# Start addresses of the matmuls' moving operands in a three-stage decoder layer: two groups of tiles are placed elsewhere

## The chip, the core and the metric

The kernel runs on one core of one Trainium2 chip, as one launch. The metric is the device time of a launch in microseconds; less is better. Engines are named as in the profile: PE is the matrix engine (PEld its weight loads), DVE the vector engine, ACT the scalar engine, POOL the general one, SP the queue that issues the loads.

## What is computed

One layer on 16 learned tokens and 256 tokens of x, width 2048, all in float32:

```
hs = concat(meta_tokens, x)                                   # 272 x 2048
f  = (silu(rms(hs) @ w_gate) * (rms(hs) @ w_up)) @ w_down      # first block, inner width 5632
hs = hs + 0.5 * rms(f)
m  = concat(sparse_attention(rms(hs) @ w_in), gated_linear_attention(rms(hs) @ w_in)) @ w_out
hs = hs + rms(m)
f  = (silu(rms(hs) @ w_gate2) * (rms(hs) @ w_up2)) @ w_down2   # second block
hs = hs + 0.5 * rms(f);  output hs[16:]                        # 256 x 2048
```

(Each rms has its own gain.) The weights are read once, some 356 MB.

## The kernel before

**Precision.** Each float32 operand is split into a rounded upper part and a lower rest (`hi`, `lo`), both float32r. A product takes three matmuls: upper weights with upper x, lower weights with upper x, upper weights with lower x (`mm3`, L137 to L141, for most of the first block and the mixer). ACT writes the upper part, DVE the lower one (`split`).

**Weights.** `load` fetches a 512 x 512 piece (1 MB) into one of three `raw` tiles over SP's queue and splits it into two `whi` and two `wlo` tiles of 4096 bytes in each partition, five buffers each. In the gate, up, input and output projections and in the first block's down projection, the weights are the stationary operand: 128 columns of 512 bytes, taken at `f * 512` bytes and `(k % 2) * 2048` bytes of such a tile. All `whi`, `wlo` and `raw` tiles begin at 96 modulo 256 bytes in their partition.

**x.** The normed activations, transposed, lie in one tile `xg` of 34816 bytes in each partition, at address 36704. For the first block and the input projections it holds 16 chunks of 272 tokens, each as 272 upper and 272 lower values, so one row of moving values is 1088 bytes and rows start 1088 bytes apart (`xs`). From the output projection on, only the 256 real tokens are needed, and `xn2` lays 16 chunks of 256 upper and 256 lower values over the same tile, `XOFF` elements from its start: rows of 1024 bytes, 1024 bytes apart (`xs2`).

**First block.** For each of 11 slices of 512 inner columns, `gate_up` (L531) streams w_gate and w_up against `xg` (272 columns a matmul), multiplies silu(gate) and up, and leaves four pairs `hhi`, `hlo` of 128 x 272; eight buffers each, so that two slices are alive. `down1` then runs w_down against them: for 16 output chunks, 4 x 3 matmuls with 272 columns, `hhi`, `hhi`, `hlo` for k = 0 to 3 (L139, L140, L141).

**Mixer.** `stream_pair` (L216) runs two index projections at once, chunk by chunk, 256 columns a matmul (L255, L256, L258, and one more of 272 columns for small weights at the end of each row of them); `stream_block` runs the others. Where 256 tokens are enough (`n == NX`, L188), upper weights meet upper and lower x in one matmul of 512 columns (L197, four in a row for k = 0 to 3), and lower weights meet upper x in one of 256 columns (L199, four in a row). With `xs`, the two halves of such a 512 are 1088 bytes apart; with `xs2` they lie end to end.

**Output projection and second block.** Both read x through `xs2`: the output projection and ten slices of gate and all but the first of up by L197 and L199, the first slice of gate and up by `stream_pair`, the last 128 output columns of the output projection by `mm3` with 256 columns. `down2` has the weights as moving operand: 512 columns of `whi`, `whi`, `wlo` against `hhi`, `hlo` (L1066 to L1068).

**Order.** The PE's order is the order of the code, written out by hand; small matmuls of the mixer are put between the large ones by a `Background` of tasks with costs. ACT and DVE are ordered by the framework.

Of the kernel before, what the change touches and what calls it, by code (L numbers as in the profile page):

```python
# [8 lines left out]
F32 = mybir.dt.float32  # L9
F32R = mybir.dt.float32r  # L10
# [5 lines left out]
P = 128  # L16
D = 2048
KC = D // P

XOFF = 64  # L20
FF = 5632
NM = 16
NX = 256
# [55 lines left out]
def layer_kernel(ctx: ExitStack, tc: tile.TileContext, a: dict, out: bass.AP):  # L79
# [130 lines left out]
    def joined(dst, bank):  # L210

        h = st.tile([P, T], F32, name="sqt", bufs=3)
        act.activation(h[:, :NX], bank[:, NX:], AF.Copy)
        return dve.tensor_tensor(dst, bank[:, :NX], h[:, :NX], op=ALU.add)
# [68 lines left out]

    xn2 = xg.rearrange("p c s t -> p (c s t)")[:, XOFF:XOFF + KC * 2 * NX]
    xn2 = xn2.rearrange("p (c s t) -> p c s t", c=KC, s=2)
# [64 lines left out]
    def sqrt_table(after):  # L350

        j = st.tile([P, 1], F32, name="junk1", bufs=1)
        act.activation(j, after, AF.Sqrt, bias=eps, scale=0.0)
# [178 lines left out]
    def gate_up(pool_, wg, wu, b, xs, sl, r, first, how=None):  # L532

        n = sl.stop - sl.start
        pair = first is not None and n == NX
        banks = first or stream_block(wg, b * BW, xs, sl, how=how)
        sg = []
        for f in range(4):
            t1 = pool_.tile([P, n], F32, name="gr", bufs=2)
            if n == NX and not first:  # L540
                joined(t1, banks[f])
                dve.tensor_tensor(t1, t1, r[:, :n], op=ALU.mult)
            else:
                dve.tensor_tensor(t1, banks[f][:, :n], r[:, :n], op=ALU.mult)
            s = pool_.tile([P, n], F32, name="sg", bufs=4)
            act.activation(s, t1, AF.Silu)
            sg.append(s)
        if b == NB - 1:
            sqrt_table(sg[3][:, 0:1])
        banks = [x[:, NX:] for x in first] if pair else stream_block(wu, b * BW, xs, sl)  # L550
        hid = []
        for f in range(4):
            if n == NX and not pair:
                t1 = pool_.tile([P, n], F32, name="gr", bufs=2)
                joined(t1, banks[f])
                dve.tensor_tensor(sg[f], t1, sg[f], op=ALU.mult)
            else:
                dve.tensor_tensor(sg[f], banks[f][:, :n], sg[f], op=ALU.mult)
            hi = pool_.tile([P, n], F32R, name="hhi", bufs=8)
            lo = pool_.tile([P, n], F32R, name="hlo", bufs=8)  # L560
            act.activation(hi, sg[f], AF.Copy)
            dve.tensor_tensor(lo, sg[f], hi.bitcast(F32), op=ALU.subtract)
            hid.append((hi, lo))
        return hid
# [44 lines left out]
    for b in range(NB):  # L609
        if b == NB - 1:  # L610

            w_in = a["w_in"]
            small_w = mixp.tile([P, 2, KC, P], F32R, name="mix")
            raw = wp.tile([P, KC, P], F32, name="raw", bufs=3)
            pool.memset(raw[:, :, 64:128], 0.0)
            for c0, n, o in ((C_IK, 80, 0), (C_GL, 16, 96)):
                nc.sync.dma_start(out=raw[:, :, o:o + n],
                                  in_=w_in[:, c0:c0 + n].rearrange("(k p) c -> p k c", p=P))
            for j in range(2):
                js = slice(8 * j, 8 * j + 8)  # L620
                split(raw[:, js], small_w[:, 0, js], small_w[:, 1, js])
        hid = gate_up(fp, a["ffn1_w_gate"], a["ffn1_w_up"], b, xs, full, begin.r, first if b == 0 else None)
        if prev is not None:
            down1(b - 1, prev)
        prev = hid
# [422 lines left out]
    with tc.tile_pool(name="ffn2", bufs=1) as fp:  # L1048
# [69 lines left out]
        for b in range(NB):  # L1118
            if b == 1:
                natural = bg.add(natural_task())  # L1120
                sums = ssf[:, 0], fp.tile([P, 8], F32, name="sse")
            hid = gate_up(fp, a["ffn2_w_gate"], a["ffn2_w_up"], b, xs2, alone, bound.r, first if b == 0 else None,
                          bound.how_next if b == 1 else None)
            if prev is not None:
                down2(b - 1, prev)
            prev = hid
# [28 lines left out]
```

## Time and profile before

| what | us |
|---|---|
| median of 3 runs (2078.28 to 2079.88) | 2079.64 |
| the profiled execution | 2079.47 |
| its span, first to last instruction | 2077.5 |
| PE busy (99% of the span) | 2060.6 |
| PEld busy | 1920.6 |
| DVE busy | 1269.1 |
| ACT busy | 942.4 |

How to read it: 2 us of the profiled execution lie outside its span. Busy time of PE counts a matmul from its start to a modelled end, and matmuls overlap: one of 272 columns is shown with 0.29 us, while the next starts some 0.125 us after it. What one costs the core is therefore the distance from its start to the next one's start. The views print starts to 0.01 us; the trace holds them to 1 ns. Means given with a count are means of those distances over all matmuls of the line with the named start address.

### The profile page before, as it was taken

To read this page: it belongs to the slowest core of one execution; us is meant where nothing else is said; L and a number is where in the kernel's file an instruction comes from. 1 tells how busy PE (TensorE), PEld (TensorE's weight loads), DVE (VectorE), ACT (ScalarE), POOL (GpSimd) and SP (SyncE) were. 2 spreads that over 40 slices of the span, in tenths; PEclk is the share of its full clock that TensorE was granted. 3 is DMA by queue.
4 is the path that set the end of the run, shared out by engine and by line. 5 is a ranking of instruction groups with operands and counts; after the bars stand their busy time and mean duration, and the time that the engine had idled before them with its cause. 6 is when DMAs were issued, how large, how long until landed. Compare 5 with 4: busy or idle time off the path is not lost.

```text
span 2077.5 us, 33335 instructions
## 1 busy us (share of the span) xinstructions
PE 2060.6 (99%) x13988; PEld 1920.6 (92%) x13988; DVE 1269.1 (61%) x1900; ACT 942.4 (45%) x1347; POOL 20.6 (1%) x36
## 2 busy tenths in 40 slices
PE   9999999999999999999999999999999999999998
PEld 9999999999999999989989998998888888888886
DVE  6455555545555657878764455776656566566657
ACT  6333433433333344664544455564444444444443
POOL 3000000000000000000000000000000000000000
PEclk9999999999999999999999999999999999999999
DMA  7555555555555654444444445465655655555653
GB/s 247 167 178 176 170 182 168 178 178 168 182 169 176 195 166 142 159 147 142 156 133 139 143 161 163 162 203 184 196 188 183 194 190 185 192 191 185 200 183 122
DMA packets 184648, 360.71 MB, mean 174 GB/s; under 512 B 9919, under 2 KB 10513, under 8 KB 184354
## 3 DMA queue, kind: packets, MB, share of 16 engines
q1 hardware_dynamic: 183552, 356.41, 52.5%
q8 instruction: 110, 1.80, 0.4%
q10 hardware_dynamic: 786, 2.14, 0.3%
q14 instruction: 40, 0.33, 0.0%
q0 software_dynamic: 160, 0.03, 0.0%
HBM read 356.46 MB, written 2.10 MB: 173 GB/s over the span
## 4 chain that ended last, share of the span: by engine, by line
PE 95%; issue 2%; DVE 1%; ACT 1%; DMA 0%; POOLq 0%; DVEq 0%; POOL 0%; ACTq 0%
PE mmb L197 20%; PE mmb L141 15%; PE mmb L139 15%; PE mmb L140 15%; PE mmb L199 10%; PE mmb L1067 4%; PE mmb L1066 4%; PE mmb L1068 4%; PE mmb L255 2%; PE mmb L256 2%; PE mmb L258 2%; PE axb L877 0%; DVE wlo L107 0%; PE axb L812 0%; PE mmb L183 0%
## 5 line engine op out<-in xcount | busy, mean ns | idle before, releaser
L107 DVE TENSOR_TENSOR wlo<-raw,whi 128x1024 fp32r<-128x1024 f32 (+1 forms) x674 | 805.2, 1218 | 582.1 <-ACT whi L106 581.0
L106 ACT ACTIVATE whi<-raw 128x1024 fp32r<-128x1024 f32 (+1 forms) x674 | 684.5, 1050 | 793.9 <-PE mmb L141 416.3
L139 PE MATMUL mmb<-xg,whi 128*128 128x272 f32 (+1 forms) x1808 | 525.0, 290 | 0.2 <-DVE qk L653 0.2
L141 PE MATMUL mmb<-xg,whi 128*128 128x272 f32 (+1 forms) x1808 | 522.0, 289 | 0.0
L140 PE MATMUL mmb<-xg,wlo 128*128 128x272 f32 (+1 forms) x1808 | 519.3, 287 | 0.0
L197 PE MATMUL mmb<-xg,whi 128*128 128x512 f32 x1840 | 506.2, 396 | 0.0
L197 PEld LDWEIGHTS mmb<-xg,whi 128*128 128x128 f32 x1840 | 314.9, 189 | 46.5 <-issue 4.0
L139 PEld LDWEIGHTS mmb<-xg,whi 128*128 128x128 f32 x1808 | 339.6, 188 | 4.8 <-issue 3.6
L141 PEld LDWEIGHTS mmb<-xg,whi 128*128 128x128 f32 x1808 | 340.5, 188 | 0.0
L140 PEld LDWEIGHTS mmb<-xg,wlo 128*128 128x128 f32 x1808 | 339.8, 188 | 0.2
L199 PEld LDWEIGHTS mmb<-xg,wlo 128*128 128x128 f32 x1840 | 281.8, 188 | 39.3
L199 PE MATMUL mmb<-xg,wlo 128*128 128x256 f32 x1840 | 292.1, 280 | 0.0
L141 PE MATMUL mmb<-hlo,whi 128*128 128x272 f32 x704 | 204.1, 290 | 0.0
L139 PE MATMUL mmb<-hhi,whi 128*128 128x272 f32 x704 | 203.8, 289 | 0.0
L140 PE MATMUL mmb<-hhi,wlo 128*128 128x272 f32 x704 | 202.0, 287 | 0.0
L1068 PE MATMUL mmb<-wlo,hhi 128*128 128x512 f32 (+1 forms) x356 | 137.8, 387 | 0.0
L1067 PE MATMUL mmb<-whi,hlo 128*128 128x512 f32 (+1 forms) x356 | 137.8, 387 | 0.0
L1066 PE MATMUL mmb<-whi,hhi 128*128 128x512 f32 (+1 forms) x356 | 137.7, 387 | 0.0
L139 PEld LDWEIGHTS mmb<-hhi,whi 128*128 128x128 f32 x704 | 133.1, 189 | 0.0
L141 PEld LDWEIGHTS mmb<-hlo,whi 128*128 128x128 f32 x704 | 132.7, 188 | 0.0
L140 PEld LDWEIGHTS mmb<-hhi,wlo 128*128 128x128 f32 x704 | 132.5, 188 | 0.0
L603 DVE TENSOR_TENSOR acc<-mmb,acc 128x272 f32<-128x272 f32 x160 | 70.2, 439 | 72.2 <-PE mmb L141 71.5
(265 smaller groups left out, 1611.2 us busy)
## 6 DMA issues: line engine op xcount, KB each, us to landing
raw<-in_ffn_w_up_dram SPq DMA_DIRECT2D x88, 1024.0 KB, 5.1
raw<-in_ffn_w_down_dram SPq DMA_DIRECT2D x88, 1024.0 KB, 5.1
raw<-in_ffn_w_gate_dram SPq DMA_DIRECT2D x87, 1024.0 KB, 5.1
raw<-in_w_in_dram SPq DMA_DIRECT2D x56, 1024.0 KB, 5.0
raw<-in_w_out_dram SPq DMA_DIRECT2D x16, 1024.0 KB, 5.0
xn<-in_x_dram SPq DMA_DIRECT2D x3, 512.0 KB, 8.3
raw<-in_ffn_w_gate_dram SPq DMA_DIRECT2D x4, 256.0 KB, 4.9
grep<-in_ffn_post_g_dram ACTq DMA_DIRECT2D x1, 1024.0 KB, 4.8
```

The source lines that it names most:

```text
L106: for ins, prior in zip((act.activation(hi, raw, AF.Copy), eng.tensor_tensor(lo, raw, hi.bitcast(F32), op=ALU.subtract)), after):
L107: eng.tensor_tensor(lo, raw, hi.bitcast(F32), op=ALU.subtract)), after):
L139: pe.matmul(ps, whi, xhi, start=start, stop=False)
L140: pe.matmul(ps, wlo, xhi, start=False, stop=False)
L141: pe.matmul(ps, whi, xlo, start=False, stop=stop)
L197: pe.matmul(wide, hi, x[k], start=ui == 0 and k == 0, stop=False)
L199: pe.matmul(wide[:, 0], wof(k, f)[1], x[k][:, 0], start=False, stop=ui == 3 and k == 3)
L255: pe.matmul(ps, hi, xh, start=c == 0 and own, stop=False, skip_group_check=True)
L603: dve.tensor_tensor(acc[:, c], ps[:, :T], acc[:, c], op=ALU.add)
L1066: pe.matmul(ps, hh[:, tk], whi, start=k == 0, stop=False)
L1067: pe.matmul(ps, hl[:, tk], whi, start=False, stop=False)
L1068: pe.matmul(ps, hh[:, tk], wlo, start=False, stop=k == 3)
```

## The change

Three places are edited. `XOFF` goes from 64 to 48 elements, so all of `xn2` lies 64 bytes lower within `xg`. In the first block (and there alone, `n != NX`) the `hhi` and `hlo` tiles are allocated with 320 elements of which 272 are used, and the two `gr` tiles with 280.

```
-XOFF = 64
+
+XOFF = 48
...
-            t1 = pool_.tile([P, n], F32, name="gr", bufs=2)
+            t1 = pool_.tile([P, n if n == NX else n + 8], F32, name="gr", bufs=2)[:, :n]
...
-            hi = pool_.tile([P, n], F32R, name="hhi", bufs=8)
-            lo = pool_.tile([P, n], F32R, name="hlo", bufs=8)
+            hi, lo = (pool_.tile([P, n if n == NX else 320], F32R, name=x, bufs=8)[:, :n] for x in ("hhi", "hlo"))
```

Start addresses in a partition, modulo 256 bytes, in the two built programs:

| operand | before | after |
|---|---|---|
| moving `hhi` and `hlo` of the first block, k = 0, 1, 2, 3 | 224, 160, 96, 32 (both alike) | 32, 32, 32, 32 |
| moving rows of `xn2` (upper and lower) | 96 | 32 |
| moving rows of `xg` through `xs`, 272 columns: upper of even, odd chunks | 96, 224 | same |
| the same, lower of even, odd chunks | 160, 32 | same |
| moving 256 tokens of `xg` through `xs`: upper of even, odd chunks | 160, 32 | same |
| the same, lower of even, odd chunks | 224, 96 | same |
| stationary `whi`, `wlo` | 96 | same |
| moving `whi`, `wlo`, stationary `hhi`, `hlo` in `down2` | 96 | same |
| the four `sg` tiles of the first block | 224, 32, 96, 160 | 32, 96, 160, 224 |
| the two `gr` tiles of the first block | 96, 160 | 96, 192 |

No instruction is added, removed or moved on any engine, and the number and sizes of the loads are the same. One wait goes: DVE writes the lower part of `xn2` in the output projection (`split_mix`, L1023), and with the chunk 64 bytes lower one of the 16 writes overlaps less of `xg` that PE still reads. On DVE, before (around it stand softmax steps on `s`, `rsm`, `mx` and the splitting of the mixer's result `mix` into `xg`):

```order
L954 TENSOR_SCALAR s<-s,rsm 128x144 [waits DVE_49]
L1023 TENSOR_TENSOR xg<-mix,xg 128x256 [waits PE_49,Activation_49] x4
L949 ISA s,mx<-axb,score_9560 128x272 [waits PE_49]
L949 ISA mx 128x1
L951 TENSOR_SCALAR nm<-mx 128x1 [waits DVE_49]
```

and after:

```order
L954 TENSOR_SCALAR s<-s,rsm 128x144 [waits DVE_49]
L1023 TENSOR_TENSOR xg<-mix,xg 128x256 [waits PE_49,Activation_49]
L1023 TENSOR_TENSOR xg<-mix,xg 128x256 [waits Activation_49]
L1023 TENSOR_TENSOR xg<-mix,xg 128x256 [waits PE_49,Activation_49] x2
L949 ISA s,mx<-axb,score_9560 128x272 [waits PE_49]
L949 ISA mx 128x1
```

The second of four such writes no longer waits for PE; its order stays.

## Rows read from the trace of the kernel before

**Rows 1.** The page: busy time, and the chain that ended last, by engine.
```profile
PE 2060.6 (99%) x13988; PEld 1920.6 (92%) x13988; DVE 1269.1 (61%) x1900; ACT 942.4 (45%) x1347; POOL 20.6 (1%) x36
PE 95%; issue 2%; DVE 1%; ACT 1%; DMA 0%; POOLq 0%; DVEq 0%; POOL 0%; ACTq 0%
```

**Rows 2.** Busy time by stretch: start:end, length, engines, granted clock, DMA share, GB/s.
```profile
42.00:811.00 769.00, 769.00 (x6118) 769.00 (x6117) 423.48 (x572) 296.32 (x360) 4.02 (x4) 1.00 0.53 175
1375.00:2020.00 645.00, 645.00 (x3440) 555.12 (x3439) 392.85 (x504) 297.00 (x402) 0.00 (x0) 1.00 0.58 189
```

**Rows 3.** Groups of PE instructions: count, busy us, mean ns, idle before.
```profile
L197 PE MATMUL mmb<-xg,whi 128*128 128x512 f32 x1840 | 506.2, 396 | 0.0
L199 PE MATMUL mmb<-xg,wlo 128*128 128x256 f32 x1840 | 292.1, 280 | 0.0
L139 PE MATMUL mmb<-hhi,whi 128*128 128x272 f32 x704 | 203.8, 289 | 0.0
L255 PE MATMUL mmb<-xg,whi 128*128 128x256 f32 x256 | 62.4, 283 | 0.7 <-ACT xg L399 0.7
```

**Rows 4.** PE in time (start, length, what), the mixer's stream_pair, two neighbouring chunks.
```profile
843.85 0.28 PE L255 MATMUL mmb<-xg,whi 128*128 128x256 f32 x1
...
845.74 0.29 PE L255 MATMUL mmb<-xg,mix 128*128 128x272 f32 x1
...
847.07 0.28 PE L255 MATMUL mmb<-xg,whi 128*128 128x256 f32 x1
...
848.89 0.29 PE L255 MATMUL mmb<-xg,mix 128*128 128x272 f32 x1
```

**Rows 5.** PE in time, the second block's stream_pair, one chunk.
```profile
1331.56 0.28 PE L255 MATMUL mmb<-xg,whi 128*128 128x256 f32 x1
...
1333.48 1.12 PE L258 MATMUL mmb<-xg,whi 128*128 128x256 f32 x8
1334.44 0.28 PE L255 MATMUL mmb<-xg,whi 128*128 128x256 f32 x1
```

**Rows 6.** PE in time, L197 and L199 in the second block.
```profile
1519.38 1.09 PE L197 MATMUL mmb<-xg,whi 128*128 128x512 f32 x4
1520.31 0.63 PE L199 MATMUL mmb<-xg,wlo 128*128 128x256 f32 x4
1520.78 1.09 PE L197 MATMUL mmb<-xg,whi 128*128 128x512 f32 x4
```

**Rows 7.** PE in time, L197 and L199 in the mixer.
```profile
1146.08 1.09 PE L197 MATMUL mmb<-xg,whi 128*128 128x512 f32 x4
1147.01 0.63 PE L199 MATMUL mmb<-xg,wlo 128*128 128x256 f32 x4
1147.47 0.60 PE L869 MATMUL axb<-ident,vt 128*16 128x128 f32 x4
```

**Rows 8.** PE in time, second block's down projection.
```profile
1500.15 0.39 PE L1066 MATMUL mmb<-whi,hhi 128*128 128x512 f32 x1
...
1501.28 0.39 PE L1068 MATMUL mmb<-wlo,hhi 128*128 128x512 f32 x1
```

**Rows 9.** PE in time, first block's down projection, one output chunk.
```profile
114.84 0.29 PE L139 MATMUL mmb<-hhi,whi 128*128 128x272 f32 x1
...
115.22 0.29 PE L139 MATMUL mmb<-hhi,whi 128*128 128x272 f32 x1
...
115.61 0.29 PE L139 MATMUL mmb<-hhi,whi 128*128 128x272 f32 x1
...
115.99 0.29 PE L139 MATMUL mmb<-hhi,whi 128*128 128x272 f32 x1
116.11 0.28 PE L140 MATMUL mmb<-hhi,wlo 128*128 128x272 f32 x1
116.23 0.29 PE L141 MATMUL mmb<-hlo,whi 128*128 128x272 f32 x1
116.36 0.29 PE L139 MATMUL mmb<-hhi,whi 128*128 128x272 f32 x1
```

**Rows 10.** PE in time, the first gate block, lower x of an odd chunk.
```profile
30.77 0.66 PE L186 MATMUL mmb<-xg,whi 128*128 128x272 f32 x4
31.27 0.38 PE L472 MATMUL axb<-ident,xn 128*128 128x128 f32 x2
```

**Rows 11.** Who waited for whom, 1375 us to the end: us, times, longest.
```profile
ACT whi L106 <- PE mmb L197: 179.5, 56, 3.8
```

## The prediction

> **What bounds the kernel now.** I read the busy times first: PE is busy for 99% of the span, and the chain that ended last runs over PE for 95% of it [rows 1]. [...] In the second block ACT waits for PE and not the reverse: 179.5 us of ACT's idle time end when PE frees a weight tile [rows 11]. So each nanosecond between the starts of two large matmuls is a nanosecond of the result, and the change, which alters addresses and no work, can act only there. The page's groups give the counts but not this distance, since their mean ns run to a modelled end [rows 3]; I took it from the starts in the timeline.
>
> **What an address costs, by the trace of before.** Two neighbouring chunks of the mixer's stream_pair are the cleanest case: the same loop, weights at the same addresses, 16 matmuls of 256 columns each. The even chunk, moving rows at 160 modulo 256, takes 845.74 - 843.85 = 1.89 us, 118.1 ns each; the odd one, at 32, takes 848.89 - 847.07 = 1.82 us, 113.8 ns each [rows 4]. [...] The second block's stream_pair, at 96, takes 1333.48 - 1331.56 = 1.92 us for 16, 120.0 ns each [rows 5]. The order 32, 160, 96 holds in every chunk of these loops (112 matmuls between two others at 32: 113.4 ns; 112 at 160: 118.3; 420 at 96: 119.6).
>
> [...]
>
> **The change part by part.**
>
> *256 columns over `xn2`, 96 to 32.* L199 has 1520 such matmuls (1840 in all [rows 3], less 320 in the mixer through `xs`). Now four take 1520.78 - 1520.31 = 0.47 us [rows 6], 118.4 ns in the mean. In the mixer, where chunks alternate between 160 and 32, four take 0.46 us [rows 7]; the ones at 32 among them show 114.3 ns (second of four, 80) and 116.1 (last of four, 42). Lower bound of the gain: all at 115.2, 3.2 ns. Upper: all at the 113.4 of stream_pair, 5.0. I take 4.0, since three of four will have neighbours at 32, as in stream_pair: 1520 x 4.0 = 6.1 us (4.9 to 7.6). The second block's stream_pair has 256 matmuls of L255 and L256 at 120.0 and 128 of L258, eight in 1334.44 - 1333.48 = 0.96 us, also 120.0 [rows 5]; at 113.8, 384 x 6.2 = 2.4 us (1.6 if L258 gains nothing). The 48 of `mm3` over `xn2` give 0.2. Together 8.7 us (6.7 to 10.2).
>
> *512 columns over `xn2`, 96 to 32.* L197, 1520 matmuls. Four take 1520.31 - 1519.38 = 0.93 us [rows 6], 232.2 ns in the mean. No row shows a 512 that lies at 32 as a whole: in the mixer the second half starts 1088 bytes after the first, so a row at 32 has its other half at 96; four there take 0.93 us too [rows 7]. That is the lower bound: no gain. The upper bound is the second block's down projection, whose 512 columns start 1501.28 - 1500.15 = 1.13 us apart over five, 226 ns (226.9 in the mean) [rows 8]; twice the 113.4 above is the same 226.8. That gives 5.4 ns or 8.2 us. The down projection has that pace with moving and stationary operand both at 96, so the residue is not all of the cause, and I take a little over half: 3.0 ns, 4.6 us (0 to 8.2).
>
> *272 columns in the first block's down projection, all to 32.* 3 x 704 = 2112 matmuls [rows 3], 126.2 ns in the mean. One output chunk shows the four residues in a row: k = 0 to 3 start at 114.84, 115.22, 115.61 and 115.99, the next chunk at 116.36 [rows 9]. In means over 176 triples, 224 takes 378.6 ns, 160 382.3, 96 380.3 and 32 372.1. Within a triple at 32 the first takes 126.8 (it follows one at 96), the second 121.0, the third 124.3 (it is followed by one at 224). Upper bound: after the change each has only neighbours at 32, as that second one: 5.2 ns x 2112 = 11.0 us. Lower bound: the four lower-x matmuls of the first gate block, a short run at 32 with 272 columns, take 31.27 - 30.77 = 0.50 us, 125 ns [rows 10]: 1.2 ns, 2.5 us. Against this row stands that its weights change column block at every matmul, where the down projection stays within one; so I lean to the other side, halfway between the whole triple at 32 (124.0) and its middle (121.0), 122.5: 3.7 x 2112 = 7.8 us (2.5 to 11.0).
>
> *Edits at nothing.* DVE's lost wait on L1023 ends no idle time of PE. The new places of `gr` and `sg` change what ACT and DVE read, both with idle time behind PE [rows 1, 2]. What is late next is nothing near: a 1 MB piece now lasts PE 16 x (232.2 + 118.4) = 5.61 us and then some 5.50, which lifts a DMA share of 0.58 [rows 2] to about 0.59, and ACT's 179.5 us of waiting for PE [rows 11] is the margin of the splits.
>
> Sum: 8.7 + 4.6 + 7.8 = 21.1 us off the profiled execution's 2079.5 gives **2058.4 us**. That execution lies 0.2 us under the median of the runs, so no correction is needed. All lower bounds together, 9.2 us, give 2070.3; all upper ones, 29.4, give 2050.1.
>
> **The rivals.**
>
> *Only the 256s gain.* The 512s keep 232 ns, as in the mixer, and the 272s settle near 126, since a row of 1088 bytes ends 64 bytes further on modulo 256 than it began. For it: [rows 7, 10]. Against: the triples at 32 in the down projection. It gives 2079.5 - 8.7 = 2070.8.
>
> *Nothing changes.* The steps seen are of the place in the loop and not of the address. Against: [rows 4], where only the chunk differs. [...]
>
> *Slower.* A residue shared by all starts removes the variety between neighbours, and each matmul meets the weight load at the same moment of its run, every time. In stream_pair that moment is the good one. If for 272 columns it is the worst that the down projection shows (130.9 ns, the first at 160 after one at 224, 176 of them) and for 512 the worst of the mixer (234.4, the first of four), the price is 4.7 x 2112 = 9.9 and 2.2 x 1520 = 3.3 us, less the 8.7 of the 256s: 4.5 us, 2084.0. It decides once the 272s settle above 130.3 ns with the 512s unchanged. Against: no matmul at 32 with a neighbour at 32 shows more than 127 ns as a rule.
>
> **How the numbers follow.** Forecast (all three parts gain) 0.72, only the 256s 0.18, nothing 0.06, slower 0.04. The prediction is the first case. The range, 2049 to 2072 us, spans that case's bounds with a microsecond at either end for the spread of the runs, and holds the second case; outside are the last two with 0.10 and some tails. A measurement of this kernel tells about 0.2%, 4.2 us, from no change: the first two cases are faster by more, 0.90; same 0.06; slower 0.04.
>
> **What the profile of the changed kernel would show.** Right: 16 matmuls of the second block's stream_pair in 1.82 us instead of 1.92; four L199 in 0.46 or less; triples of the first block's down projection all alike, 0.36 to 0.37 us, the block's 272s over `xg` at their old pace; second-block down at 226 to 227 ns as now. The 512s are the open term: four in 0.93 us means that it is void, 0.91 that it is full. Wrong: gaps on PE that now wait for `whi` or `wlo`, triples at 0.38 us or more, or a stream_pair of the second block at 0.12 us a matmul in spite of its new address.

## The result: faster, by 0.6%

| | before | after |
|---|---|---|
| median, us | 2079.15 (6 runs, 2077.89 to 2080.78) | 2066.57 (6 runs, 2065.20 to 2067.15) |
| span of the profiled execution, us | 2077.5 | 2064.7 |

The ratio after to before is 0.9937, 95% interval [0.9926, 0.9947]: 12.6 us less, where 21.1 was forecast. The time lies inside the stated range, nearer to its slow end than to its middle.

The page of the changed kernel: busy time by engine, and the chain that ended last by engine, to be laid beside [rows 1].

```profile
PE 2047.0 (99%) x13988; PEld 1907.1 (92%) x13988; DVE 1269.1 (61%) x1900; ACT 942.1 (46%) x1347; POOL 20.6 (1%) x36
PE 97%; DVE 2%; ACT 1%; issue 0%; DMA 0%; DVEq 0%; ACTq 0%
```

The same number of matmuls, 13.6 us less of PE and 13.5 of its weight loads; the other engines kept their busy time: DVE 1269.1 before and after, ACT 942.4 and 942.1. The same two stretches by engine (start:end, length, busy time and count of PE, PEld, DVE, ACT, POOL, granted clock, DMA share, GB/s), after:

```profile
42.00:811.00 769.00, 768.73 (x6159) 768.31 (x6158) 428.16 (x580) 297.47 (x362) 4.62 (x4) 1.00 0.54 175
1370.00:2010.00 640.00, 640.00 (x3437) 550.26 (x3436) 393.32 (x503) 296.00 (x401) 0.00 (x0) 1.00 0.58 190
```

From 42 to 811 us PE starts 6159 matmuls where it started 6118 [rows 2]; in the second block 3437 in 640 us against 3440 in 645. The granted clock was 1.00 in both stretches of both kernels, so this is pace and not clock.

Now the pace itself, PE in time (start, length, engine, line, what, count; a line number is one higher than before up to line 559). First the first block's down projection:

```profile
115.02 0.28 PE L140 MATMUL mmb<-hhi,whi 128*128 128x272 f32 x1
...
116.50 0.28 PE L140 MATMUL mmb<-hhi,whi 128*128 128x272 f32 x1
```

Twelve matmuls in 1.48 us, 123.3 ns each, against 116.36 - 114.84 = 1.52 us in [rows 9]. Then the second block's L198 and L200 (L197 and L199 of before) by turns:

```profile
1507.92 1.09 PE L198 MATMUL mmb<-xg,whi 128*128 128x512 f32 x4
1508.85 0.62 PE L200 MATMUL mmb<-xg,wlo 128*128 128x256 f32 x4
1509.30 1.09 PE L198 MATMUL mmb<-xg,whi 128*128 128x512 f32 x4
1510.23 0.62 PE L200 MATMUL mmb<-xg,wlo 128*128 128x256 f32 x4
1510.69 1.09 PE L198 MATMUL mmb<-xg,whi 128*128 128x512 f32 x4
```

Four 256s take 0.45 and 0.46 us where they took 0.47 [rows 6]; four 512s take 0.93 as before. And one chunk of the second block's stream_pair:

```profile
1327.43 0.28 PE L256 MATMUL mmb<-xg,whi 128*128 128x256 f32 x1
...
1329.32 1.10 PE L259 MATMUL mmb<-xg,whi 128*128 128x256 f32 x8
1330.26 0.28 PE L256 MATMUL mmb<-xg,whi 128*128 128x256 f32 x1
```

1.89 us for 16, 118.1 ns, against 1.92 in [rows 5] and the 1.82 that the same residue shows in the mixer [rows 4].

Summed over all matmuls of each kind, by the distances between starts:

| matmuls | count | before, us | after, us | gain | forecast |
|---|---|---|---|---|---|
| first block's down projection, 272 | 2112 | 266.5 (126.1 ns) | 260.7 (123.4) | 5.8 | 7.8 |
| L199 over `xn2`, 256 | 1520 | 180.1 (118.5) | 174.3 (114.7) | 5.7 | 6.1 |
| L197 over `xn2`, 512 | 1520 | 354.4 (232.1) | 354.5 (232.1) | -0.2 | 4.6 |
| second block's stream_pair, 256 | 384 | 46.3 | 45.4 | 0.9 | 2.4 |
| the 48 of `mm3` over `xn2` | 48 | 6.4 | 6.1 | 0.2 | 0.2 |

Their sum is 12.5 us of the 12.8 by which the two spans differ. (Gains are taken before rounding. A mean in brackets leaves out distances of 300 ns and more: one in the first block's down projection, and those of the 17 L197 that stand right behind smaller matmuls.)

### The profile page after: what moved, and what is told of

Its sections match the earlier page's. It is cut to its first block, busy times and chain, and to the rows that moved or that the text cites. A ratio compares the mean times of both kernels' runs of the same rounds, so it can differ in the third digit from the quotient of the medians.

```text
span 2064.7 us, 33334 instructions
## 1 busy us (share of the span) xinstructions
PE 2047.0 (99%) x13988; PEld 1907.1 (92%) x13988; DVE 1269.1 (61%) x1900; ACT 942.1 (46%) x1347; POOL 20.6 (1%) x36
## 4 chain that ended last, share of the span: by engine, by line
PE 97%; DVE 2%; ACT 1%; issue 0%; DMA 0%; DVEq 0%; ACTq 0%
PE mmb L198 21%; PE mmb L142 15%; PE mmb L140 15%; PE mmb L141 15%; PE mmb L200 10%; PE mmb L1067 4%; PE mmb L1066 4%; PE mmb L1068 4%; PE mmb L256 2%; PE mmb L257 2%; PE mmb L259 2%; PE axb L812 1%; PE axb L877 0%; DVE wlo L108 0%; PE mmb L184 0%; PE axb L875 0%
## 5 line engine op out<-in xcount | busy, mean ns | idle before, releaser
L198 PE MATMUL mmb<-xg,whi 128*128 128x512 f32 x1840 | 506.2, 397 | 0.0
L198 PEld LDWEIGHTS mmb<-xg,whi 128*128 128x128 f32 x1840 | 312.6, 188 | 44.5 <-issue 4.0
L200 PEld LDWEIGHTS mmb<-xg,wlo 128*128 128x128 f32 x1840 | 279.9, 188 | 41.4
L200 PE MATMUL mmb<-xg,wlo 128*128 128x256 f32 x1840 | 286.6, 278 | 0.0
```

The lines of the kernel that those rows point to most:

```text
L198: pe.matmul(wide, hi, x[k], start=ui == 0 and k == 0, stop=False)
L200: pe.matmul(wide[:, 0], wof(k, f)[1], x[k][:, 0], start=False, stop=ui == 3 and k == 3)
```

## Experiments

The theory to be tested: the pace of a matmul is set by the address of its moving row, through its place relative to the weights that are loaded meanwhile, and each part of the change acts by itself. (Of the 14119 weight loads, 13335 start 2 to 4 ns after the start of a matmul in the trace of before, and 13338 in that of the changed kernel.) The rivals are named with each run. Where a table gives means by place, they are of distances between starts, over all matmuls of that kind in the run's trace.

### Do the parts add?

`e1_x_only` has the first line of the change alone, `e2_hid_only` the rest.

```
e1: -XOFF = 64
    +XOFF = 48
e2: -t1 = pool_.tile([P, n], F32, name="gr", bufs=2)
    +t1 = pool_.tile([P, n if n == NX else n + 8], F32, name="gr", bufs=2)[:, :n]
    -hi = pool_.tile([P, n], F32R, name="hhi", bufs=8)          (and hlo)
    +hi = pool_.tile([P, n if n == NX else 320], F32R, name="hhi", bufs=8)[:, :n]
```

> XOFF alone is 48, the first block's tiles are as before. Theory (each part acts by itself through the pace of its own matmuls): L199 falls from 118.5 to about 114.7 ns a matmul, L197 stays at 233, the second block's stream_pair falls from 120 to 118, the first block keeps its 126.2 ns a matmul in the down projection: 6.8 us off, some 2072. Rival (the parts act together, through what precedes them): less or more than that, with other paces than in the changed kernel.

> The first block's tiles alone are moved, XOFF is 64 as before. Theory (the parts add): the first block's down projection falls from 126.2 to 123.4 ns a matmul, 5.8 us, some 2073; all matmuls over xn2 keep their paces of before. Rival (the parts act together): something else moves as well.

`e1` took 2071.59 us (the kernel before, run beside it, 2079.21; ratio 0.9962, interval [0.9949, 0.9975]), `e2` 2073.79 (0.9974, [0.9964, 0.9985]). Gains of 7.6 and 5.4 us make 13.0, against 12.6 for both. In `e2` the down projection has 260.7 us, the same as in the changed kernel, and L197, L199 and stream_pair stand where they stood before. In `e1` L199 has 174.3 us and L197 354.5, again the numbers of the changed kernel. The parts add, with one exception: the second block's stream_pair, at the same addresses as in the changed kernel, ran at another pace. One chunk of it in `e1`:

```profile
1330.10 0.28 PE L255 MATMUL mmb<-xg,whi 128*128 128x256 f32 x1
...
1331.91 1.07 PE L258 MATMUL mmb<-xg,whi 128*128 128x256 f32 x8
1332.82 0.28 PE L255 MATMUL mmb<-xg,whi 128*128 128x256 f32 x1
```

1.81 us for 16, 113.1 ns, in chunks 0 to 14, and 118 in chunk 15; in the changed kernel 118 in all but chunk 14, which had 113. So 32 modulo 256 allows at least two steady paces, and which one holds is not set by the address.

### The row's own address, or its place relative to the weights?

`e3_weights_up` leaves `xg`, `xn2` and `XOFF` as they were and moves the weights. The 64 bytes of padding move the `raw`, `whi` and `wlo` tiles and everything that is allocated above them, the first block's own tiles among it:

```
-wp = ctx.enter_context(tc.tile_pool(name="wp", bufs=1))
+wp = ctx.enter_context(tc.tile_pool(name="wp", bufs=1)); wp.tile([P, 16], F32, name="pad")
```

> Addresses of xg and xn2 as before (xn2 at 96), but 64 unused bytes ahead of the raw, whi and wlo tiles put the stationary weights at 160 modulo 256 in place of 96; the first block's own tiles move up by 64 with them. Theory A (what counts is where the moving row starts relative to the weights that are loaded beside it): xn2 now stands 64 below the weights, as in the changed kernel, so L199 goes to about 114.7 ns and the second block's stream_pair to 118; the first block's down projection, where both move, keeps 126.2; the 272s over xg change their pace. Theory B (the moving row's own address counts): L199 stays at 118.5 ns, stream_pair at 120, the time at 2079.

2072.38 us (before 2079.21; 0.9965, [0.9951, 0.9979]). PE in time, second block:

```profile
1511.66 1.09 PE L197 MATMUL mmb<-xg,whi 128*128 128x512 f32 x4
1512.59 0.62 PE L199 MATMUL mmb<-xg,wlo 128*128 128x256 f32 x4
1513.04 1.09 PE L197 MATMUL mmb<-xg,whi 128*128 128x512 f32 x4
```

0.45 us for four 256s whose rows never moved. The eight places of a group of L197 and L199 have 226.1, 235.7, 230.9, 235.7, 118.5, 113.4, 113.4 and 113.5 ns; in the changed kernel they have 226.0, 235.6, 230.9, 235.7, 118.5, 113.5, 113.4 and 113.5. It is the same pattern to a tenth of a nanosecond. The mixer shows the reverse: the odd chunk of [rows 4], with rows still at 32 but now 128 bytes from the weights, takes 1.90 us where it took 1.82:

```profile
845.94 0.28 PE L255 MATMUL mmb<-xg,whi 128*128 128x256 f32 x1
...
847.84 0.29 PE L255 MATMUL mmb<-xg,mix 128*128 128x272 f32 x1
```

The first block's down projection kept 126.1 ns, as its tiles moved with the weights, and its pattern moved along: the triple of 126.8, 121.0 and 124.3 ns that stood at 32 before now stands at 96 (126.7, 120.8, 124.2). Theory B falls: what counts is the distance between the moving row and the weights, modulo 256 bytes. With the moving rows in place, other addresses of the weights changed the mean pace of the 256s from 118.5 to 114.7 ns. Whether the row or the load is held up, no run shows.

`e4_x_256_up` has `XOFF = 112`, 256 bytes above the change's place.

> XOFF alone is 112: xn2 is at 32 modulo 256 as with 48, one step of 256 bytes higher. Theory (the address counts modulo 256): the same paces as with 48, L199 about 114.7 ns with 118.5, 113.4, 113.4, 113.3 in its four places, L197 at 233, stream_pair at 118, some 2072. Rival (a larger period, or the overlap with xg): other paces.

2071.78 us in one run; 226.0, 235.6, 230.9, 235.7, 118.5, 113.5, 113.4, 113.5 ns in the eight places. So a step of 256 bytes leaves the pace where the changed kernel has it. One of 128 does not: 64 below and 64 above the weights differ in the map that follows, with 114.7 and 115.6 ns for the 256s, 232.1 and 230.4 for the 512s. (Its stream_pair ran at 113 but for the last chunk, like that of `e1`.)

### A map of distances

Four kernels, each with another distance for `xn2` and, since the parts add, another for the hidden tiles: `XOFF` 80, 32, 56 and 40, and `gr` tiles larger by 16, 24, 0 and 8 elements.

```
c1: XOFF = 80, gr n + 16      c2: XOFF = 32, gr n + 24
c3: XOFF = 56, gr n           c4: XOFF = 40, gr n + 8       (hhi, hlo 320 wide in all)
```

> XOFF 80 puts xn2 at 160, 64 bytes above the weights (96); the first block's hidden tiles are all at 96, level with the weights. Theory (the place relative to the weights sets the pace, and 64 below is the good place): L199 near the 118 ns that rows 64 above the weights show in the mixer, the second block's stream_pair near 118; the down projection of the first block near the 126.8 that a row at 96 between two others at 96 shows. Time near 2079. Rival (what matters is that all starts are alike): both gain as in the changed kernel, 115 and 123.4 ns, time near 2067.

> XOFF 32 puts xn2 at 224, 128 bytes from the weights; the hidden tiles are all at 160, 64 above. Theory (the place relative to the weights): L199 near 119.8 ns, as L258 at 224 in the mixer, stream_pair near 120; the first block's down projection near the 124.9 of a row at 160 between two others there, 2.5 us less than before. Time near 2077. Rival (all alike is enough): 115 and 123.4, near 2067.

> XOFF 56 puts xn2 at 64, 32 bytes below the weights; the hidden tiles are all at 224, 128 from the weights. Theory (the place relative to the weights, in steps of 64): 32 below lies between the places of 118.5 and 114.7 for L199, no row shows which it takes; the hidden tiles near the 122.9 ns of a row at 224 between two others there, 6.8 us less than before. Time between 2065 and 2073. Rival (only 64 below is good): hidden tiles at 126 and no gain there.

> XOFF 40 puts xn2 at 0, 96 bytes below the weights; the hidden tiles are at 32 as in the changed kernel. Theory (the place relative to the weights): no row shows 96 below; if the good place is a stretch around 64 below, L199 stays near 114.7 and the time near 2067; if it is 64 below alone, L199 goes back to 118 or more and the time to 2073. The term that failed in the prediction, the 512s at 233 ns, may lie lower here than at 64 below; each nanosecond is 1.5 us.

One run each: 2070.98, 2081.99, 2078.92 and 2075.81 us, with 2082.89 for the kernel before beside them. Single times differ by a few microseconds here, so I go by the paces:

| `xn2`, bytes from the weights | 8 places, ns in sum | 512, mean | 256, mean | stream_pair, by chunk |
|---|---|---|---|---|
| -96 (c4) | 1409.2 | 233.5 | 118.8 | 117, last 120 |
| -64 (after) | 1387.1 | 232.1 | 114.7 | 118 or 113 |
| -32 (c3) | 1403.3 | 231.6 | 119.2 | 118 |
| 0 (before) | 1402.2 | 232.1 | 118.5 | 120 |
| +64 (c1) | 1383.7 | 230.4 | 115.6 | 118 |
| 128 (c2) | 1404.1 | 233.4 | 117.7 | 118 to 120 |

| hidden tiles, bytes from the weights | 272, mean ns |
|---|---|
| -64, all alike (after, c4) | 123.4 |
| 0, all alike (c1) | 125.3 |
| +64, all alike (c2) | 126.7 |
| 128, all alike (c3) | 126.7 |
| one of each (before) | 126.1 |

That all rows are alike is not what helps: at two of the four uniform places the down projection is slower than with one of each. For `xn2` the good place is narrow, 32 bytes to either side of 64 below lose all of the gain, and 64 above, which I had expected to do nothing for `xn2`, is as good. (There 115.6 is the mean of two kinds of group that take turns, one with 256s near 113 ns, one near 118; each group takes some 1383.) What rows of before showed between two equal neighbours (121.0, 126.8, 124.9, 122.9 ns at -64, 0, +64, 128) was no measure of the steady pace.

`e7_160_32` puts `xn2` there (`XOFF = 80`) and keeps the hidden tiles of the change.

> The changed kernel with XOFF 80: xn2 64 bytes above the weights, the hidden tiles 64 below as in the changed kernel. Theory (the parts add): the 512s at 230.4 and the 256s at 115.5 ns as with XOFF 80 before, the first block's down projection at 123.4, the time some 1.3 us under the changed kernel, 2065. Rival (the gain of that single look was a better run of the first 512s, not of the address): the same as the changed kernel within a microsecond, with the 512s at 232.

2064.96 us (before 2078.87; 0.9935, [0.9919, 0.9952]); 512s at 230.4, 256s at 115.6, down projection 123.4, as expected. By its paces it is a little better than the change, 3.4 ns in each of some 380 groups, 1.3 us; the intervals of the two ratios overlap almost wholly, so the runs do not tell them apart.

### Why do the 512s not gain?

`e6_runs_of_16` is the changed kernel with the 512s of a step in one run and the 256s in another.

```
 for f in range(nf):
     ... 4 of 512 for k in range(4)
-    for k in range(0 if f in plain else 4):
-        pe.matmul(wide[:, 0], wof(k, f)[1], x[k][:, 0], ...)
+for f in range(nf if xs is xs2 else 0):
+    for k in range(0 if f in plain else 4):
+        pe.matmul(banks[f][:, :NX], wof(k, f)[1], xs(4 * u + k)[:, 0, sl], ...)
```

> The changed kernel, and over xn2 the order within a step of 512 rows is changed: first the four output blocks' 16 matmuls of 512 columns, then their 16 of 256 columns, in place of four and four by turns. Same work and same addresses. Theory A (the 512s fail to gain because each switch between 512 and 256 columns, eight a step, shifts the weight load against the moving row): long runs settle, the 512s near the 226.8 ns of the second block's down projection and the 256s near 113.4 in all places, up to 8 us under the changed kernel, some 2059. Theory B (the 512s over xn2 do not gain because of their own addresses, each with another row and other weights): they stay near 232 on average in the long run too, the time near 2066.

2075.67 us (before 2078.87; 0.9985, [0.9976, 0.9994]), 9 us slower than the change. Two runs of 16, PE in time:

```profile
1513.44 3.89 PE L197 MATMUL mmb<-xg,whi 128*128 128x512 f32 x16
1517.17 1.99 PE L203 MATMUL mmb<-xg,wlo 128*128 128x256 f32 x16
1519.00 3.89 PE L197 MATMUL mmb<-xg,whi 128*128 128x512 f32 x16
```

16 of 512 take 3.73 us, 233.1 ns each, and 16 of 256 take 1.83, 114.4. In the run that follows a down projection, as the first one here, all the 512s take 233 or 234 ns; in the others they go by turns at 231 and 235 ns from the second place to the run's end. At this distance theory A falls: a long run does settle, but at 233.3 and not at 226.8.

Nor is theory B right, by the trace of the kernel before. Its first four 512s after a down projection:

```profile
1512.16 0.39 PE L1068 MATMUL mmb<-wlo,hhi 128*128 128x512 f32 x1
1512.39 1.07 PE L197 MATMUL mmb<-xg,whi 128*128 128x512 f32 x4
1513.29 0.64 PE L199 MATMUL mmb<-xg,wlo 128*128 128x256 f32 x4
```

They take 0.90 us, and 226.7 ns each over all nine such places: the down projection's own pace, with another row and other weights each time. From the next group on, 256s have come between, and the four places have 233.7, 234.1, 231.9 and 228.6 ns in the mean. In the changed kernel the first four take 0.93 us, 233.3 each:

```profile
1503.75 1.09 PE L198 MATMUL mmb<-xg,whi 128*128 128x512 f32 x4
1504.68 0.63 PE L200 MATMUL mmb<-xg,wlo 128*128 128x256 f32 x4
```

So for 512 columns too the distance sets the pace of a run: 226.7 ns level with the weights, 233.3 at 64 below. For 256 columns it is 120.0 [rows 5] and 113.3 (`e1`). One of each makes 346.7 ns at either distance. A group of the changed kernel takes that for each pair (1387.1 / 4 = 346.8), a group of before 350.6. By these rows, what the change took away in these groups is what the turns between the two widths cost level with the weights, 3.8 ns a pair. Runs of 16 level with the weights, which would test this, were not made.

The 9 us that `e6` lost are another thing. I read them so: all four banks now end late together, and the output projection pays for it. Waits of PE in that kernel (us in total, times, longest):

```profile
PE axb L315 <- DVE sq L365: 3.5, 1, 3.5
PE mmb L197 <- DVE mix L218: 2.5, 4, 0.8
```

These two are 6.0 us. The first stands in the list of the changed kernel too, with 0.5 (its L312), the second does not: 5.5 of the 9 us are in these waits.

`e8_narrow` takes the 512s away: over `xn2` each product is three matmuls of 256, on the addresses of the change.

```
+plain = range(nf) if xs is xs2 else plain
-joined(t1, banks[f])
-dve.tensor_tensor(t1, t1, r[:, :n], op=ALU.mult)
+dve.tensor_tensor(t1, banks[f][:, :n], r[:, :n], op=ALU.mult)       (up and w_out likewise)
```

> The changed kernel, and over xn2 every product is three matmuls of 256 columns (upper, lower, upper weights) in place of one of 512 and one of 256; ACT and DVE no longer add the two halves. Theory (the gain is lost in the 512s, and rows of 256 at 64 below the weights hold 113.4 ns whatever their order): as in the 16 triples of the output projection's last block in the changed kernel, 340.0 ns a triple against 346.8 for 512 and 256 there, 1520 x 6.8 = 10.3 us under the changed kernel, some 2056. Rival (each row used twice in a row settles at the 117.8 of the second block's stream_pair): 353 a triple, some 2076. Second rival (1520 more weight loads cost time of their own): slower than the changed kernel with PE's starts further apart than 118 ns.

`e9_narrow_96` does the same on the addresses of before.

> The kernel before with the same three matmuls of 256 columns over xn2, all addresses as before (xn2 at 96, level with the weights). Theory (the address decides what the form is worth): 119.5 ns a matmul as in the kernel before, 358.4 a triple against 350.6 for 512 and 256, 1520 x 7.8 = 12 us slower than before, some 2091. Rival (three 256s are the better form at any address): faster than before.

`e8` took 2071.28 us (before 2079.42; 0.9961, [0.9947, 0.9975]): faster than before, slower than the change. Both the theory and its first rival came true, one after the other. PE in time, 30 matmuls at 1409 us and 30 at 1455 us:

```profile
1409.00 0.28 PE L139 MATMUL mmb<-xg,whi 128*128 128x256 f32 x1
...
1412.40 0.39 PE L1058 MATMUL mmb<-whi,hhi 128*128 128x512 f32 x1
...
1455.02 0.28 PE L139 MATMUL mmb<-xg,whi 128*128 128x256 f32 x1
...
1458.55 0.28 PE L139 MATMUL mmb<-xg,whi 128*128 128x256 f32 x1
```

3.40 us, 113.3 ns each, and 3.53 us, 117.7 each: same loop, same addresses. Of the first 384 triples 364 take 340 to 346 ns, and all 1152 later ones 353 or 354; the step comes once, between 1412 and 1426 us, where a stretch of the down projection stands between two gate blocks, and the slow pace then holds to the end through every such stretch. With 340 throughout the kernel would have been 1152 x 13.3 = 15 us faster, 2056; that is an estimate from these rows.

`e9` took 2093.53 us in one run, 14 slower than before:

```profile
1454.83 0.28 PE L139 MATMUL mmb<-xg,whi 128*128 128x256 f32 x1
...
1457.71 0.28 PE L139 MATMUL mmb<-xg,whi 128*128 128x256 f32 x1
```

24 matmuls in 2.88 us, 120.0 ns each, and so in 1486 of 1536 triples. Level with the weights this form shows no second steady pace.

## Why the prediction was right, and where its sum was off

**The bound** was right: PE stayed busy (99% of the span, and 640.00 of the second block's 640 us), and the time between starts came off the result. The five kinds of matmul account for 12.5 us of it. Nothing late took its place.

**The mechanism** was right in its direction, and `e3` made it sharper: it is the distance to the weights. The rival that nothing changes, since the steps seen are of the place in the loop, fell with [rows 4] and again with `e3`. But the case that was given 0.72, in which all three parts gain, did not come as it was told: two of them gained. The range had room for it, as that case's lower bound put the 512s at nothing.

**256s over `xn2`** were sized well: 3.8 ns against 4.0. Three of four places went to 113.5 or less, as taken from stream_pair; the first, after a 512, came to 118.5.

**512s over `xn2`** were the step that failed: 3.0 ns forecast, none measured. The lower bound, read from the mixer's 0.93 us for four [rows 7], was right. The upper one, borrowed from the down projection [rows 8], was not within reach: those rows lie level with their stationary operand, and 64 bytes below it 512s settle at 233.3 (`e6`). The first of four did fall from 233.7 to 226.0, but the four together kept their time, the fourth rising from 228.6 to 235.7. That 512s over `xn2` held 226.7 level with the weights, until 256s came between, stood in the trace of before, and the prediction did not read it. At all six distances the mean by turns lay between 230.4 and 233.5.

**272s** gained 2.7 ns where 3.7 was forecast. I had leaned to the middle of the triple (121.0) as the pace with like neighbours; the steady mean is 123.4, near that of the whole triple (124.0). The row that spoke against it, 125 ns [rows 10], was the better warning.

**The second block's stream_pair** gained 0.9 and not 2.4, because it ran at 118 where the mixer's chunk at the same distance runs at 113.8. I took one pace per address for granted; `e1`, `e4` and `e8` show two, and what chooses between them is open.

**"Only the 256s gain"** would have been 2070.8. It was right on the 512s and wrong on the 272s; the 2066.6 that came lies between it and the forecast, nearer to the rival. **"Slower"** needed the 272s to settle above 130.3 ns. The worst steady mean that the map shows for them is 126.7 (`c2`, `c3`), at other distances than the change's; for 256 columns it is 120.0 (`e9`).

## What to carry to other kernels

In a stream of matmuls that PE bounds, measure the distance from start to start by operand address before anything else is tuned: here the same 256 columns took 113.4 to 120.0 ns by where the moving row started relative to the weights loaded beside it, modulo 256 bytes, and padding that puts the rows at a good distance was worth 0.6% with the same instructions. Take the pace for a forecast from a long run of the very shape at that distance, since values next to a change of address (121.0 ns against 123.4), or from another distance (226.8 against 232.1), did not carry over, and count what a change of width costs between the runs. And check the form again after the address: three matmuls of 256 cost 360 ns a product at one distance and 340 or 353 at another, against 351 and 347 for one of 512 and one of 256.

## What the runs showed of the hardware that I had not expected

- The address of the weights that are loaded beside a running matmul bears on its pace: moving them by 64 bytes, with what lies above them (`e3`), gave the same 5.7 us on L199 as moving the rows.
- Long runs have paces of their own by distance: 256 columns 113.3 or 117.8 ns at 64 below, 120.0 level (stream_pair, `e8`, `e9`); 512 columns 233.3 at 64 below (`e6`), 226.7 level (L197 after a down projection, before). The highest and the lowest differ by 6.7 ns for both widths. At the other distances of the map runs of 256 lie mostly between, at 117 to 119.
- At 64 bytes below the weights two paces of 256 columns are each steady: in `e8` 364 of the first 384 triples take 340 to 346 ns and all 1152 later ones 353 or 354; and the step from one to the other comes where other matmuls stand between (a few small ones in stream_pair, a down projection in `e8`). What decides it was not tried.
